# Interleaving the first two column groups of an encoder block's input projection, and moving its norm to sums per token

## The chip, the cores and the metric

The kernel runs on one core of one Trainium2 chip. The metric is the device time of one execution in microseconds (us): 1427.27 as the median of three runs (1427.24 to 1427.72).

## What is computed

One layer of an encoder block for 256 tokens of width 2048, in float32. The part that matters here is its first line, the RMSNorm and the input projection, of which the three hyena parts of 1024 columns each come first, and the small network that makes the hyena filter:

```python
h = rms_norm(x, g_mix)                        # 256 x 2048
proj = einsum('bld,de->ble', h, w_in)         # w_in: 2048 x 10240
q, k, v, hy, gates = split(proj, ...)
hy = dwconv3(hy, hy_conv_w, hy_conv_b)        # width 3 along the tokens
x0, x1, hv = split(hy, 3)                     # 1024 channels each
kern = hyena_filters(...)                     # three layers sin(freq * (h @ w + b)), then @ w4, times a decay
u = x1 * hv
y_hy = x0 * (long_conv(u, kern) + u * hy_d)
...                                           # attention, gates, merge, w_out, gated MLP, last norm
```

## The kernel before

**A stream of weights.** Nearly all of the work is one list of *chunks* (`chunks`, filled by `add_group`, line 113). A chunk is up to 1024 columns of weights on 128 partitions: for a hyena group two *K-tiles* (128 rows of x's 2048 each) of 512 columns. The loop at the end of the kernel (lines 899 to 924) does for chunk `i`: start the load of chunk `i+5` into a slab `wr` (five buffers, on SP's queue), prepare chunk `i+2`, and emit the matmuls of chunk `i`. To prepare is to split the slab into a high half `wh` (a cast on ACT, line 99) and a low half `wl` (a subtraction on DVE, line 66), three buffers each. Each engine works through its own instructions in the order in which they were emitted.

**A hyena group** is 512 output channels over all 16 K-tiles of x, channel-major: four PSUM banks (`acc{i}_0` to `_3`), each with 128 channels on the partitions. Per K-tile and bank there are two matmuls: `wh` against x's high and low half in one (512 columns), `wl` against x's high half (256 columns) into the bank's second half; `emit_mm`, line 159. When the last chunk of a group is emitted, its four *steps* go on a list (`pending`), and `flush` takes one from it per chunk: `merged_sum` (line 187) adds a bank's halves (ACT copies one as `lo`, DVE adds), the sum is multiplied by `rstd`, and `dwconv` makes the convolution (one ACT operation, two on DVE). There are six such groups: for each half of the channels the parts 1 (x1), 2 (hv) and 0 (x0). PSUM has eight banks, handed out in rotation to groups, steps and background work alike. A group has 8 chunks; the very first has 12, eight with a single K-tile and four with two.

**x and its norm.** With each chunk of the first group its K-tiles of x are loaded, scaled by the gain and split into `xg` (`split_scaled`, one operation on ACT, one on DVE at line 78). For every two K-tiles ACT squares x (`x_norm_sq`, line 228) and GpSimd adds the squares to `sqacc`. Behind the group's last chunk `x_norm_end` (line 236) sums over the partitions with a matmul by ones into `rs_ps`, and `rsqrt_chain` (line 199) makes `rstd`, the factor of each token, on all partitions. The projection itself runs on x without that factor; it is multiplied in later.

**The filter in the background.** `filter_gen` (line 284) is a generator. From chunk 16 the loop calls it 0.9 times per chunk (`pace`). Its pieces in order: loads of its tables and the split of the `dft` matrices; the split of `w4` (cast on ACT, subtraction on DVE); three layers, each a small matmul into `f_ps{l}`, an ACT operation that makes `fy`, five DVE operations, and Sin on ACT, with two empty pieces behind each; a split; then the matmuls `h_ps...` with `w4`, followed by the work for the filter's spectrum.

Of the kernel before, what the change touches and what calls it, by code (L numbers as in the profile page):

```python
# [17 lines left out]
P = 128  # L18
# [28 lines left out]
def block(ctx: ExitStack, tc: tile.TileContext, a, out):  # L47
# [14 lines left out]
    def etile(tag, name, shape=(P, T), bufs=None):  # L62
        return ev.tile(list(shape), F32, tag=tag, name=name, bufs=bufs)
# [16 lines left out]
    def ts(o, x, s1, s2, op0, op1=None):  # L80
        if op1 is None:
            nc.vector.tensor_scalar(out=o, in0=x, scalar1=s1, scalar2=None, op0=op0)
        else:
            nc.vector.tensor_scalar(out=o, in0=x, scalar1=s1, scalar2=s2, op0=op0, op1=op1)
# [99 lines left out]
                    mm(o, xl, wh[:, k, :], False, end and k == n - 1)  # L184
        return g if end else None

    def merged_sum(pt, name):
        lo = etile("lo", f"lo_{name}")
        nc.scalar.copy(out=lo, in_=pt[:, T:])  # L189
        s = etile("sum", f"s_{name}")  # L190
        add(s, pt[:, :T], lo)
        return s

    def dwconv(dst, u, c0):
        act(dst, u, AF.Identity, scale=pk[:, c0 + 1:c0 + 2], bias=pk[:, c0 + 3:c0 + 4])
        stt(dst[:, 1:], u[:, :T - 1], pk[:, c0:c0 + 1], dst[:, 1:], ALU.mult, ALU.add)
        stt(dst[:, :T - 1], u[:, 1:], pk[:, c0 + 2:c0 + 3], dst[:, :T - 1], ALU.mult, ALU.add)

    def rsqrt_chain(dst, src, n, name):

        b = etile("sq", f"rq_{name}", (P, 2, T), 2)
        ms, t = b[:, 0, :n], b[:, 1, :n]
        ts(ms, src, 1.0 / D, EPS, ALU.mult, ALU.add)
        act(t, ms, AF.Sqrt)
        nc.vector.reciprocal(out=dst, in_=t)
        mul(t, dst, dst)
        mul(t, t, ms)
        ts(t, t, -0.5, 1.5, ALU.mult, ALU.add)
        mul(dst, dst, t)


    xT = [s8(f"xT{i}", [P, 8, T]) for i in range(2)]
# [13 lines left out]
        return xT[kk // 8][:, kk % 8, :]  # L226

    def x_norm_sq(j):
        sq = etile("sq", f"sq{j}", (P, 2, T), 2)
        act(sq, xT[j // 4][:, (j % 4) * 2:(j % 4) * 2 + 2, :], AF.Square)  # L230
        if j == 0:
            nc.gpsimd.tensor_copy(out=sqacc, in_=sq)
        else:
            nc.gpsimd.tensor_tensor(out=sqacc, in0=sqacc, in1=sq, op=ALU.add)

    def x_norm_end():
        pt = bank("rs_ps")
        nc.gpsimd.tensor_tensor(out=sqacc[:, 0, :], in0=sqacc[:, 0, :], in1=sqacc[:, 1, :], op=ALU.add)
        mm(pt[:, :T], ones, sqacc[:, 0, :], True, True)
        rsqrt_chain(rstd, pt[:, :T], T, "x")  # L240
        d = etile("cv", "rtok")
        for t in range(2):
            nc.vector.tensor_tensor_reduce(out=d[:, :P], in0=rstd[:, t * P:(t + 1) * P], in1=ident, scale=1.0,
                                           scalar=0.0, op0=ALU.mult, op1=ALU.add,
                                           accum_out=rstd_tok[:, t:t + 1])

    def xop(kk):
        return xg[kk // 4][:, kk % 4, :]
# [4 lines left out]
    def hy_groups():  # L253
        def eo(x):
            return x.rearrange("p (m e) -> p e m", e=2)

        def step(part, half, c):
            def f(pts):
                ct = half * 4 + c
                if part == 1 and c == 0:  # L260
                    hy["x1"] = s8(f"hy_x1_{half}", [P, 4, T])
                    if half == 0:
                        hy["u"] = s8("hy_u", [P, 8, 2, P])
                        hy["x0"] = s8("hy_x0", [P, 8, T])
                s = merged_sum(pts[c], f"hy{part}_{ct}")
                mul(s, s, rstd)
                c0 = C_HYC + 4 * (part * 8 + ct)
                if part == 0:
                    dwconv(hy["x0"][:, ct, :], s, c0)
                elif part == 1:  # L270
                    dwconv(hy["x1"][:, c, :], s, c0)
                else:
                    v = etile("cv", f"hv{ct}")
                    dwconv(v, s, c0)
                    mul(hy["u"][:, ct, :, :], eo(hy["x1"][:, c, :]), eo(v))
            return f

        for half in range(2):
            for part in (1, 2, 0):
                first = part == 1 and half == 0  # L280
                add_group(a["w_in"][6 + part * 2 + half], KT, 512, xop, [step(part, half, c) for c in range(4)],
                          sizes=[1] * 8 + [2] * 4 if first else None)

    def filter_gen():
        raw = s8("dft_raw", [P, 8, P])
# [546 lines left out]
        while bg:  # L832
            run_bg(1)

    pair, pace = [False], [0.9, 0.0]

    def setp(pr, pc):
        pair[0], pace[0] = pr, pc
# [60 lines left out]
    for i in range(n):  # L899
        if i in events:  # L900
            flush(9)
            for fn in events[i]:
                fn()
        if i + LOAD < n:
            load(i + LOAD)
        if i + SPLIT < n:
            prep(i + SPLIT)
        if i == 6:
            nc.sync.dma_start(out=pk[:, C_HYC:], in_=a["pk"][:, C_HYC:])
        if i == 16:  # L910
            bg.append(filter_gen())
        g = emit_mm(i)
        if i == 11:
            x_norm_end()
        flush(1)
        pace[1] += pace[0]
        while pace[1] >= 1:
            pace[1] -= 1
            run_bg(1)
        if g is not None:  # L920
            pts = g.pts
            g.pts = None
            pending += [lambda f=f, pts=pts: f(pts) for f in g.steps]
            flush(1)
    while pending:
        pending.pop(0)()
    assert not bg
# [108 lines left out]
```

## Time and profile before

| | us |
|---|---|
| median of three runs | 1427.27 |
| the profiled execution, its own time | 1428.48 |
| its span, first to last instruction | 1426.2 |
| PE (TensorE's matmuls) busy | 1412.1 |
| PEld (its weight loads, beside PE) busy | 1214.2 |
| DVE (VectorE) busy | 991.6 |
| ACT (ScalarE) busy | 782.4 |
| POOL (GpSimd) busy | 19.2 |
| granted TensorE clock, mean | 0.998 |

Busy times are sums over the whole span, so they tell which engine is full and not where it stands idle; the chain of waits and the timelines tell that. SP only issues transfers. In rows of the trace `out<-in` are the names of tiles with buffer numbers left out, `128x512` is partitions x elements, and `[0.98 <-ACT wh]` at a row's end is the idle time of the engine ahead of it and what ended that. DVE and ACT records that follow each other overlap by some 0.08 us: an operation's record ends after the next one's has begun.

### The profile page before, as it was taken

What the parts mean: (1) busy time and instruction counts of PE and PEld (TensorE: products, weight loads), DVE (VectorE), ACT (ScalarE), POOL (GpSimd) and SP (SyncE); (2) the same over time, 40 slices, a digit from 0 to 9 for tenths busy, and PEclk for the clock granted to TensorE, in tenths of its full rate; (3) what the DMA queues carried; (4) which work ended last, traced back from release to release, by engine and by line L of the source; (5) the groups of instructions that cost most, each with busy time, mean ns of one, the idle gap of its engine ahead of it and who ended that gap; (6) DMA issues with size and microseconds to landing.
All of it is one profiled execution on the core that took longest, in us unless ns stands there. A gap on an engine that the chain in (4) does not pass through costs nothing.

```text
span 1426.2 us, 20169 instructions
## 1 busy us (share of the span) xinstructions
PE 1412.1 (99%) x7588; PEld 1214.2 (85%) x7588; DVE 991.6 (70%) x1532; ACT 782.4 (55%) x1171; POOL 19.2 (1%) x35
## 2 busy tenths in 40 slices
PE   8999999999999999999999999999999999999997
PEld 6888888888888888888888888888888888888897
DVE  7988877755688765755677787777777776545464
ACT  7665554443576666444566566565655654434354
POOL 3000000000000000000000000000000000000000
PEclk9999999999999999999999999999999999999999
DMA  8755555566555557565556666666666666666683
GB/s 276 240 185 156 164 175 176 165 224 195 187 163 161 165 174 239 177 189 180 184 188 191 191 191 191 188 189 190 191 190 192 190 190 221 195 193 192 192 262 123
DMA packets 77866, 271.88 MB, mean 191 GB/s; under 512 B 8960, under 2 KB 12065, under 8 KB 77257
## 3 DMA queue, kind: packets, MB, share of 16 engines
q1 hardware_dynamic: 77048, 269.54, 60.3%
q8 instruction: 59, 0.97, 0.3%
q10 hardware_dynamic: 720, 1.07, 0.2%
q14 instruction: 39, 0.31, 0.1%
HBM read 268.45 MB, written 2.11 MB: 190 GB/s over the span
## 4 chain that ended last, share of the span: by engine, by line
PE 98%; DMA 1%; DVE 1%; issue 0%; SPq 0%; ACT 0%; DVEq 0%; ACTq 0%
PE acc L90 94%; DMA wr<-in_w_in_dram 1%; PE s_ps L90 1%; PE y_ps L90 1%; PE o_ps L90 0%; DVE wl L66 0%; PE h_ps L90 0%; PE k_ps L90 0%; PE mt L475 0%; PE wt_ps L621 0%; PE xt L475 0%; PE ua_ps L90 0%; PE ub_ps L90 0%; PE ut_ps L376 0%; PE ot_ps L668 0%
## 5 line engine op out<-in xcount | busy, mean ns | idle before, releaser
L66 DVE TENSOR_TENSOR wl<-wr,wh 128x1024 fp32r<-128x1024 f32 (+1 forms) x495 | 602.4, 1218 | 378.0 <-ACT wh L99 376.1
L99 ACT CAST wh<-wr 128x1024 fp32r<-128x1024 f32 (+1 forms) x495 | 516.9, 1045 | 521.1 <-PE acc L90 474.5
L90 PE MATMUL acc<-xg,wh 128*128 128x512 f32 x2048 | 715.0, 395 | 1.5 <-ACT wh L99 1.3
L90 PE MATMUL acc<-xg,wl 128*128 128x256 f32 x2048 | 567.1, 278 | 2.7 <-DVE wl L66 2.5
L90 PEld LDWEIGHTS acc<-xg,wh 128*128 128x128 f32 x2048 | 383.6, 188 | 91.0 <-ACT wh L99 2.2
L90 PEld LDWEIGHTS acc<-xg,wl 128*128 128x128 f32 x2048 | 384.5, 188 | 6.4 <-DVE wl L66 5.0
L90 PE MATMUL acc<-wh,m 128*128 128x512 f32 (+1 forms) x832 | 218.2, 350 | 0.0
L90 PE MATMUL acc<-wh,xg 128*128 128x512 f32 x640 | 205.2, 393 | 0.0
L90 PEld LDWEIGHTS acc<-wh,m 128*128 128x128 f32 x832 | 146.9, 189 | 20.5
L90 PE MATMUL acc<-wl,m 128*128 128x512 f32 (+1 forms) x416 | 145.7, 350 | 0.0
L90 PEld LDWEIGHTS acc<-wh,xg 128*128 128x128 f32 x640 | 120.2, 188 | 24.6 <-issue 0.2
L90 PE MATMUL acc<-wl,xg 128*128 128x512 f32 x320 | 124.8, 390 | 0.0
L90 PEld LDWEIGHTS acc<-wl,m 128*128 128x128 f32 x416 | 78.7, 189 | 10.5 <-DVE wl L66 0.2
L90 PE MATMUL acc<-wh,mg 128*128 128x512 f32 x256 | 81.2, 393 | 0.0
L90 PEld LDWEIGHTS acc<-wl,xg 128*128 128x128 f32 x320 | 60.2, 188 | 11.7 <-DVE wl L66 0.2
L90 PEld LDWEIGHTS acc<-wh,mg 128*128 128x128 f32 x256 | 48.1, 188 | 9.9
L90 PE MATMUL acc<-wl,mg 128*128 128x512 f32 x128 | 49.8, 389 | 0.0
L90 PE MATMUL acc<-wh,att 128*128 128x512 f32 x128 | 41.4, 395 | 0.0
L78 DVE SCALAR_TENSOR_TENSOR sg<-s_up,pk,sg 128x255 f32<-128x255 f32 x88 | 39.5, 480 | 1.0 <-ACT sg L87 0.2
L78 DVE SCALAR_TENSOR_TENSOR vv<-s_up,pk,vv 128x255 f32<-128x255 f32 x88 | 39.3, 478 | 0.4
L90 PE MATMUL acc<-wh,yhy 128*128 128x512 f32 x128 | 39.6, 389 | 0.0
L189 ACT COPY lo_up<-acc 128x256 f32<-128x256 f32 x88 | 32.1, 365 | 10.7 <-PE acc L90 9.3
(198 smaller groups left out, 970.6 us busy)
## 6 DMA issues: line engine op xcount, KB each, us to landing
wr<-in_w_up_dram SPq DMA_DIRECT2D x176, 512.0 KB, 4.2
wr<-in_w_in_dram SPq DMA_DIRECT2D x156, 512.0 KB, 3.8
wr<-in_w_down_dram SPq DMA_DIRECT2D x66, 512.0 KB, 4.3
wr<-in_w_out_dram SPq DMA_DIRECT2D x32, 512.0 KB, 3.6
wr<-in_w_down_t_dram SPq DMA_DIRECT2D x28, 512.0 KB, 4.7
wr<-in_w_hb_dram SPq DMA_DIRECT2D x16, 512.0 KB, 4.4
wr<-in_w_ab_dram SPq DMA_DIRECT2D x16, 512.0 KB, 4.2
wr<-in_w_in_dram SPq DMA_DIRECT2D x8, 256.0 KB, 5.1
```

The source lines that it names most:

```text
L66: nc.vector.tensor_tensor(out=o, in0=x, in1=y, op=op)
L78: nc.vector.scalar_tensor_tensor(out=o, in0=x, scalar=s, in1=y, op0=op0, op1=op1)
L90: nc.tensor.matmul(o, lhsT=lhsT, rhs=rhs, start=start, stop=stop)
L99: nc.scalar.copy(out=hi, in_=x)
L189: nc.scalar.copy(out=lo, in_=pt[:, T:])
```

## The change

Part 1 and part 2 of the first half of the channels are now the first two groups, and their chunks alternate in the list: chunk 0 of the one, chunk 0 of the other, and so on, each group with four chunks of one K-tile and six of two (20 chunks in all). The eight banks of PSUM hold both groups. Since a pair of chunks shares its K-tiles, x is loaded and split with every other chunk. The remaining order is part 0, then parts 1, 2 and 0 of the second half.

The squares are added by DVE, GpSimd adds none. When the two groups end, their sums are *parked* without the norm's factor, in places of `hy_x1` and `hy_u` that are free until later (up to four steps at once while the chunk number is under 20). Then comes the norm as a step (`x_norm_chain`): two f32 matmuls of 128 columns give the sums per token on the partitions, the arithmetic is done on 128x2 values, and DVE writes two diagonal matrices into `sqacc`; two steps later `x_norm_spread` brings them to all partitions by a matmul of 256 columns and a copy on ACT. The convolutions of the parked sums follow as steps. The filter starts at chunk 23 and is called 1.15 times per chunk.

```diff
--- before.py
+++ after.py
@@ -184,10 +184,10 @@
                     mm(o, xl, wh[:, k, :], False, end and k == n - 1)
         return g if end else None
 
-    def merged_sum(pt, name):
+    def merged_sum(pt, name, s=None):
         lo = etile("lo", f"lo_{name}")
         nc.scalar.copy(out=lo, in_=pt[:, T:])
-        s = etile("sum", f"s_{name}")
+        s = etile("sum", f"s_{name}") if s is None else s
         add(s, pt[:, :T], lo)
         return s
 
@@ -195,18 +195,6 @@
         act(dst, u, AF.Identity, scale=pk[:, c0 + 1:c0 + 2], bias=pk[:, c0 + 3:c0 + 4])
         stt(dst[:, 1:], u[:, :T - 1], pk[:, c0:c0 + 1], dst[:, 1:], ALU.mult, ALU.add)
         stt(dst[:, :T - 1], u[:, 1:], pk[:, c0 + 2:c0 + 3], dst[:, :T - 1], ALU.mult, ALU.add)
-
-    def rsqrt_chain(dst, src, n, name):
-
-        b = etile("sq", f"rq_{name}", (P, 2, T), 2)
-        ms, t = b[:, 0, :n], b[:, 1, :n]
-        ts(ms, src, 1.0 / D, EPS, ALU.mult, ALU.add)
-        act(t, ms, AF.Sqrt)
-        nc.vector.reciprocal(out=dst, in_=t)
-        mul(t, dst, dst)
-        mul(t, t, ms)
-        ts(t, t, -0.5, 1.5, ALU.mult, ALU.add)
-        mul(dst, dst, t)
 
 
     xT = [s8(f"xT{i}", [P, 8, T]) for i in range(2)]
@@ -226,23 +214,33 @@
         return xT[kk // 8][:, kk % 8, :]
 
     def x_norm_sq(j):
-        sq = etile("sq", f"sq{j}", (P, 2, T), 2)
+        sq = sqacc if j == 0 else etile("sq", f"sq{j}", (P, 2, T), 2)
         act(sq, xT[j // 4][:, (j % 4) * 2:(j % 4) * 2 + 2, :], AF.Square)
-        if j == 0:
-            nc.gpsimd.tensor_copy(out=sqacc, in_=sq)
-        else:
-            nc.gpsimd.tensor_tensor(out=sqacc, in0=sqacc, in1=sq, op=ALU.add)
-
-    def x_norm_end():
+        if j:
+            add(sqacc, sqacc, sq)
+        if j == 7:
+            add(sqacc[:, 0, :], sqacc[:, 0, :], sqacc[:, 1, :])
+
+    def x_norm_chain(pts):
         pt = bank("rs_ps")
-        nc.gpsimd.tensor_tensor(out=sqacc[:, 0, :], in0=sqacc[:, 0, :], in1=sqacc[:, 1, :], op=ALU.add)
+        for t in range(2):
+            mm(pt[:, t * P:(t + 1) * P], sqacc[:, 0, t * P:(t + 1) * P], ones, True, True)
+        rq = cp.tile([P, 2, 2], F32, name="rq")
+        ms, y = rq[:, 0, :], rq[:, 1, :]
+        ts(ms, pt[:, 0:2 * P:P], 1.0 / D, EPS, ALU.mult, ALU.add)
+        act(y, ms, AF.Sqrt)
+        nc.vector.reciprocal(out=rstd_tok, in_=y)
+        mul(y, rstd_tok, rstd_tok)
+        mul(y, y, ms)
+        ts(y, y, -0.5, 1.5, ALU.mult, ALU.add)
+        mul(rstd_tok, rstd_tok, y)
+        for t in range(2):
+            ts(sqacc[:, 0, t * P:(t + 1) * P], ident, rstd_tok[:, t:t + 1], None, ALU.mult)
+
+    def x_norm_spread(pts):
+        pt = bank("rd_ps")
         mm(pt[:, :T], ones, sqacc[:, 0, :], True, True)
-        rsqrt_chain(rstd, pt[:, :T], T, "x")
-        d = etile("cv", "rtok")
-        for t in range(2):
-            nc.vector.tensor_tensor_reduce(out=d[:, :P], in0=rstd[:, t * P:(t + 1) * P], in1=ident, scale=1.0,
-                                           scalar=0.0, op0=ALU.mult, op1=ALU.add,
-                                           accum_out=rstd_tok[:, t:t + 1])
+        nc.scalar.copy(out=rstd, in_=pt[:, :T])
 
     def xop(kk):
         return xg[kk // 4][:, kk % 4, :]
@@ -254,15 +252,24 @@
         def eo(x):
             return x.rearrange("p (m e) -> p e m", e=2)
 
-        def step(part, half, c):
+        def parked(part, c):
+            return hy["x1"][:, 4 + c, :] if part == 1 else hy["u"][:, 4 + c, :, :].rearrange("p e m -> p (e m)")
+
+        def park(part, c):
+            def f(pts):
+                if part == 1 and c == 0:
+                    hy["x1"] = s8("hy_x1_0", [P, 8, T])
+                    hy["u"] = s8("hy_u", [P, 8, 2, P])
+                    hy["x0"] = s8("hy_x0", [P, 8, T])
+                merged_sum(pts[c], f"hy{part}_{c}", parked(part, c))
+            return f
+
+        def step(part, half, c, early=False):
             def f(pts):
                 ct = half * 4 + c
-                if part == 1 and c == 0:
+                if part == 1 and c == 0 and not early:
                     hy["x1"] = s8(f"hy_x1_{half}", [P, 4, T])
-                    if half == 0:
-                        hy["u"] = s8("hy_u", [P, 8, 2, P])
-                        hy["x0"] = s8("hy_x0", [P, 8, T])
-                s = merged_sum(pts[c], f"hy{part}_{ct}")
+                s = parked(part, c) if early else merged_sum(pts[c], f"hy{part}_{ct}")
                 mul(s, s, rstd)
                 c0 = C_HYC + 4 * (part * 8 + ct)
                 if part == 0:
@@ -275,11 +282,15 @@
                     mul(hy["u"][:, ct, :, :], eo(hy["x1"][:, c, :]), eo(v))
             return f
 
-        for half in range(2):
-            for part in (1, 2, 0):
-                first = part == 1 and half == 0
-                add_group(a["w_in"][6 + part * 2 + half], KT, 512, xop, [step(part, half, c) for c in range(4)],
-                          sizes=[1] * 8 + [2] * 4 if first else None)
+        sizes = [1] * 4 + [2] * 6
+        add_group(a["w_in"][8], KT, 512, xop, [park(1, c) for c in range(4)], sizes=sizes)
+        add_group(a["w_in"][10], KT, 512, xop,
+                  [park(2, c) for c in range(4)] + [x_norm_chain, lambda pts: None, x_norm_spread]
+                  + [step(part, 0, c, True) for part in (1, 2) for c in range(4)], sizes=sizes)
+        n0 = len(sizes)
+        chunks[:] = [c for pr in zip(chunks[:n0], chunks[n0:]) for c in pr]
+        for part, half in ((0, 0), (1, 1), (2, 1), (0, 1)):
+            add_group(a["w_in"][6 + part * 2 + half], KT, 512, xop, [step(part, half, c) for c in range(4)])
 
     def filter_gen():
         raw = s8("dft_raw", [P, 8, P])
@@ -832,7 +843,7 @@
         while bg:
             run_bg(1)
 
-    pair, pace = [False], [0.9, 0.0]
+    pair, pace = [False], [1.15, 0.0]
 
     def setp(pr, pc):
         pair[0], pace[0] = pr, pc
@@ -907,11 +918,9 @@
             prep(i + SPLIT)
         if i == 6:
             nc.sync.dma_start(out=pk[:, C_HYC:], in_=a["pk"][:, C_HYC:])
-        if i == 16:
+        if i == 23:
             bg.append(filter_gen())
         g = emit_mm(i)
-        if i == 11:
-            x_norm_end()
         flush(1)
         pace[1] += pace[0]
         while pace[1] >= 1:
@@ -921,7 +930,7 @@
             pts = g.pts
             g.pts = None
             pending += [lambda f=f, pts=pts: f(pts) for f in g.steps]
-            flush(1)
+            flush(4 if i < 20 else 1)
     while pending:
         pending.pop(0)()
     assert not bg
```

Three places where the order of an engine's instructions changes. The rows are the engine's instructions in its own order; a number behind a name is that of the chunk (`wl5`), K-tiles group (`xg1`) or bank, and the last number of a name only tells tiles apart.

DVE at the start, from the low half of chunk 3 on, before:

```order
L66 TENSOR_TENSOR wl3_162<-wr3_102,wh3_161 128x512
L78 SCALAR_TENSOR_TENSOR xg1_78<-xT0_75,pk_72,xg1_78 128x256
L66 TENSOR_TENSOR wl4_182<-wr4_105,wh4_181 128x512
L78 SCALAR_TENSOR_TENSOR xg1_78<-xT0_75,pk_72,xg1_78 128x256
L66 TENSOR_TENSOR wl5_199<-wr5_136,wh5_198 128x512
L78 SCALAR_TENSOR_TENSOR xg1_78<-xT0_75,pk_72,xg1_78 128x256
L66 TENSOR_TENSOR wl6_219<-wr6_157,wh6_218 128x512
```

and from chunk 4's on after the change:

```order
L66 TENSOR_TENSOR wl4_173<-wr4_103,wh4_172 128x512
L66 TENSOR_TENSOR wl5_188<-wr5_128,wh5_187 128x512
L78 SCALAR_TENSOR_TENSOR xg0_77<-xT0_75,pk_72,xg0_77 128x256
L66 TENSOR_TENSOR sqacc_81<-sqacc_81,sq1_207 128x512
L66 TENSOR_TENSOR wl6_204<-wr6_150,wh6_203 128x512
L66 TENSOR_TENSOR wl7_222<-wr7_168,wh7_221 128x512
L78 SCALAR_TENSOR_TENSOR xg1_78<-xT0_75,pk_72,xg1_78 128x256 x2
L66 TENSOR_TENSOR sqacc_81<-sqacc_81,sq2_243 128x512
L66 TENSOR_TENSOR wl8_240<-wr8_185,wh8_239 128x1024
```

Before, an operation on `xg` (a K-tile of x) stands between any two low halves. After, two low halves follow each other, and the additions into `sqacc` stand among them, where before GpSimd had them.

ACT around the filter's first layer, before (`fy0` and `fy1` are the arguments of the first and second Sin, `fsm` takes Sin's result, `hv` are convolutions):

```order
L87 ACTIVATE fy0_629<-f_ps0_627,fsm_562,pk_72 128x256
L189 COPY lo_hy2_0_659<-acc12_0_427 128x256
L189 COPY lo_hy2_1_695<-acc12_1_428 128x256
L189 COPY lo_hy2_2_727<-acc12_2_429 128x256
L189 COPY lo_hy2_3_759<-acc12_3_430 128x256
L99 CAST wh22_671<-wr22_579 128x1024
L87 ACTIVATE hv0_664<-s_hy2_0_661,pk_72 128x256
L87 ACT_TABLE_LOAD
L87 ACTIVATE fsm_562<-fy0_629 128x256
L99 CAST wh23_707<-wr23_604 128x1024
L87 ACTIVATE hv1_700<-s_hy2_1_697,pk_72 128x256
L87 ACTIVATE hv2_732<-s_hy2_2_729,pk_72 128x256
```

and after:

```order
L87 ACTIVATE fy0_790<-f_ps0_788,fsm_715,pk_72 128x256
L99 CAST wh29_826<-wr29_732 128x1024
L189 COPY lo_hy0_0_950<-acc20_0_606 128x256
L189 COPY lo_hy0_1_990<-acc20_1_607 128x256
L189 COPY lo_hy0_2_1020<-acc20_2_608 128x256
L99 CAST wh30_870<-wr30_761 128x1024
L87 ACT_TABLE_LOAD
L87 ACTIVATE fsm_715<-fy0_790 128x256
L87 ACTIVATE hv1_863<-hy_u_552,pk_72 128x256
L87 ACTIVATE hv2_895<-hy_u_552,pk_72 128x256
L87 ACTIVATE fy1_854<-f_ps1_852,fsm_715,pk_72 128x256
```

Before, between `fy0` and Sin stand four copies of bank halves, the cast of chunk 22, a convolution and the table load; behind Sin the casts go on (23, and below these rows 24 and 25) until `fy1`. After, between `fy0` and Sin stand the casts of chunks 29 and 30 with three copies and the table load, and between Sin and `fy1` two convolutions and no cast.

PE around the second layer's matmul `f_ps1`, before:

```order
L90 MATMUL acc20_3_678<-xg1_78,wl22_672 128x256
L90 MATMUL acc20_3_678<-xg1_78,wh22_671 128x512
L90 MATMUL acc20_3_678<-xg1_78,wl22_672 128x256
L90 MATMUL f_ps1_769<-fsm_562 128x256
L90 MATMUL acc20_0_675<-xg1_78,wh23_707 128x512
L90 MATMUL acc20_0_675<-xg1_78,wl23_708 128x256
L90 MATMUL acc20_0_675<-xg1_78,wh23_707 128x512
L90 MATMUL acc20_0_675<-xg1_78,wl23_708 128x256
L90 MATMUL acc20_1_676<-xg1_78,wh23_707 128x512
```

and after:

```order
L90 MATMUL acc20_3_609<-xg3_80,wh27_763 128x512
L90 MATMUL acc20_3_609<-xg3_80,wl27_764 128x256
L90 MATMUL acc20_3_609<-xg3_80,wh27_763 128x512
L90 MATMUL acc20_3_609<-xg3_80,wl27_764 128x256
L90 MATMUL f_ps1_852<-fsm_715 128x256
L90 MATMUL acc28_0_874<-xg0_77,wh28_800 128x512
L90 MATMUL acc28_0_874<-xg0_77,wl28_801 128x256
L90 MATMUL acc28_0_874<-xg0_77,wh28_800 128x512
L90 MATMUL acc28_0_874<-xg0_77,wl28_801 128x256
L90 MATMUL acc28_1_875<-xg0_77,wh28_800 128x512
```

The matmul stood behind chunk 22 and ahead of chunk 23; it now stands behind chunk 27 and ahead of chunk 28. The first layer's matmul `f_ps0` stands behind chunk 18 before and behind chunk 25 after, so that four chunks lay between the two, and two do now.

## Rows read from the trace of the kernel before

**Rows 1.** The page, section 1: busy us, share of the span, instructions, by engine.

```profile
PE 1412.1 (99%) x7588; PEld 1214.2 (85%) x7588; DVE 991.6 (70%) x1532; ACT 782.4 (55%) x1171; POOL 19.2 (1%) x35
```

**Rows 2.** Waits of PE over the span: us in total, times, longest.

```profile
PE acc L90 <- DVE wl L66: 2.5, 3, 1.4
```

**Rows 3.** The chain that ended last: start us, us, what (x of instructions).

```profile
4.03 6.35 DMA wr<-in_w_in_dram
...
11.85 5.19 DMA wr<-in_w_in_dram
...
34.21 0.43 PE rs_ps L90 x2
34.65 19.42 PE acc L90 x112
...
54.50 11.10 PE acc L90 x64
...
66.03 8.33 PE acc L90 x48
...
74.78 13.87 PE acc L90 x80
...
697.73 719.95 PE acc L90 x4072
```

**Rows 4.** Timeline of PE at the start: start us, us, engine, line, operation, [idle before].

```profile
4.97 1.29 PE L90 MATMUL acc<-xg,wh 128*128 128x512 f32 x4
...
11.15 0.98 PE L90 MATMUL acc<-xg,wh 128*128 128x512 f32 x3 [0.83 <-ACT wh L99]
```

**Rows 5.** Timelines of GpSimd (POOL) and DVE, 19 to 30 us.

```profile
19.66 1.32 POOL L234 TENSOR_TENSOR sqacc<-sqacc,sq 128x512 f32<-128x512 f32 x1 [0.50 <-ACT sq L87]
...
19.76 2.30 DVE L66 TENSOR_TENSOR wl<-wr,wh 128x1024 fp32r<-128x1024 f32 x1
...
24.96 2.38 DVE L78 SCALAR_TENSOR_TENSOR xg<-xT,pk,xg 128x256 fp32r<-128x256 f32 x2
...
28.40 0.87 DVE L78 SCALAR_TENSOR_TENSOR xg<-xT,pk,xg 128x256 fp32r<-128x256 f32 x2
29.19 1.21 DVE L66 TENSOR_TENSOR wl<-wr,wh 128x1024 fp32r<-128x1024 f32 x1
```

**Rows 6.** Timeline of ACT at the start, and one window of all engines (clock, DMA).

```profile
10.48 0.62 ACT L99 CAST wh<-wr 128x512 fp32r<-128x512 f32 x1 [0.98 <-DMA wr<-in_w_in_dram]
...
20.00:22.00 2.00, 0.75 (x4) 0.27 (x2) 2.00 (x2) 2.00 (x5) 0.98 (x1) 1.00 1.04 403
```

**Rows 7.** Groups by form, 0 to 160 us: busy us, mean ns of one, idle before.

```profile
L66 DVE TENSOR_TENSOR k<-k_ps,kt 128x512 f32<-128x512 f32 x8 | 5.5, 687 | 2.4 <-PE k_ps L90 2.4
...
L78 DVE SCALAR_TENSOR_TENSOR hy_x<-s_hy,pk,hy_x 128x255 f32<-128x255 f32 x24 | 10.7, 478 | 0.0
...
L66 DVE TENSOR_TENSOR s_hy<-s_hy,rstd 128x256 f32<-128x256 f32 x22 | 8.9, 418 | 0.1
...
L84 DVE TENSOR_SCALAR fy<-fy 128x256 f32<-128x256 f32 x6 | 1.7, 286 | 0.2 <-ACT fy L87 0.2
```

**Rows 8.** Timeline of ACT around the filter's layers.

```profile
60.81 1.28 ACT L87 ACT_TABLE_LOAD   x1
62.10 0.42 ACT L87 ACTIVATE fsm<-fy 128x256 f32<-128x256 f32 x1
...
77.48 1.05 ACT L99 CAST wh<-wr 128x1024 fp32r<-128x1024 f32 x1 [1.66 <-PE acc L90]
78.44 0.41 ACT L87 ACTIVATE fsm<-fy 128x256 f32<-128x256 f32 x1
```

**Rows 9.** Timelines of SP's queue and ACT, the filter's transfers.

```profile
43.11 0.43 SPq L286 DMA_DIRECT2D dft_raw<-in_dft_dram  x1
...
54.42 1.05 ACT L99 CAST w<-w4r 128x1024 fp32r<-128x1024 f32 x1 [1.17 <-DMA w4r<-in_hy_f_w_dram]
```

**Rows 10.** Window of all engines behind the last matmul.

```profile
1422.00:1424.00 2.00, 0.00 (x0) 0.00 (x0) 0.00 (x0) 0.00 (x0) 0.00 (x0) 0.50 1.09 351
```


## The prediction

> **What bounds the kernel now.** I read the page's engine line first: PE is busy for 1412.1 of a span of 1426.2 us [rows 1], so only time in which PE stands still, or works that it is given or spared, can move the result. The list of waits says where it stands: its largest entry is the low half of a weight slab, `wl`, made by DVE [rows 2]. The chain in order of time says when: up to 34.21 it passes through transfers, ACT and DVE, and from there on it is matmuls alone [rows 3]. So the start is the one stage with something to win. Its size: 112 matmuls (7 chunks of 16) took 19.42 us [rows 3], so a chunk of two K-tiles costs 2.775 us and a K-tile 1.387. The first group has 16 K-tiles, 22.2 us; its first matmul starts at 4.97 [rows 4] and the norm's matmul `rs_ps`, next behind its last chunk, at 34.21 [rows 3]. The start loses 34.21 - 4.97 - 22.2 = 7.05 us.
>
> Two things make that loss. Early, transfers: ACT waited 0.98 us for chunk 3's slab at 10.48 [rows 6], which had taken 6.35 us from its issue at 4.03 [rows 3]. Later, DVE: while GpSimd adds one square tile (19.66 to 20.98), a `wl` of 1024 columns takes 2.30 us instead of 1.21, and a pair of `xg` operations 2.38 instead of 0.87 [rows 5]. With GpSimd adding, a round of two K-tiles took DVE some 3 us, more than PE's 2.775.
>
> **What the change does to the start.** Two groups now share every K-tile of x, so PE has 5.55 us of work for a pair of K-tiles where it had 2.775. DVE must do for it: the `xg` pair 0.79 (0.87 less the 0.08 or so by which records in a row overlap), two `wl` at 1.14, and one addition of squares of 512 columns at 0.61 (0.687 less the overlap [rows 7]): 3.7 us of 5.55. The eight additions that move to it (some 4.6 us in all) are hidden by that slack; without it they would cost what they take. ACT needs 3.3 us of the 5.55 (two casts at 1.05, two scaled copies at 0.41, a Square of 512 columns at about the 0.62 of a cast of that size, less the overlap [rows 6, 8]). The transfers must bring 1.31 MB in 5.55 us, 236 GB/s; the queue has moved 403 GB/s in this kernel [rows 6]. So the steady part should run at PE's pace.
>
> Three chunks should still be late. Chunk 0 needs the same two transfers as before and starts at 4.97. Chunk 2's slab is the fifth transfer instead of the sixth but behind more bytes: 0.4 us. Chunk 4's slab is now the eighth; the eighth landed just before 10.48 [rows 3, 6], its cast takes 0.62, and PE wants it at about 10.9: 0.2 us. Chunk 8 is the first of 512 KB; its load waits for the buffer that `wl3` frees, at about 10, takes 5.19 to 6.35 us [rows 3], and then a cast of 1.05 and a `wl` of 1.21 (a second matmul already needs it): ready at 17.5 to 18.6, where PE is free at about 16.7 and has one matmul of 0.2 to do first. I take the later end, since 256 KB of x go ahead of it: 1.7 us. Together 2.3 us stay lost; bounds 0.7 (all of it early) and 4.7 (2.0 us for the first chunks of each group, by which chunk 3 was late before, 11.15 [rows 4] against 4.97 + 3 x 1.387, and chunk 8's at less than half its price).
>
> **What it adds on PE.** The norm's 256 columns in plain f32 cost 0.43 us [rows 3]. Now two of 128 columns (0.43 together) and one of 256 to spread the result: +0.43 us. The tiny operations on 128x2 and the two diagonals lie on DVE and ACT between the two, and two chunks (5.55 us) cover them; the removed work on 256 columns gives DVE back time that PE never waited for after 34.21 [rows 3].
>
> Parking the eight sums puts eight ACT copies and eight DVE additions behind the last two chunks. Group A's banks are wanted again at chunk 20, one chunk (2.775 us) after its last matmul; the four copies need 1.3 us (0.41 each less the overlap [rows 8]) and the additions keep pace, so I cost this at nothing. Without that cover it would be up to 1.5 us. The bank of every later group is free by its turn, as the eight are handed out in rotation.
>
> **What moves later: the filter.** filter_gen starts at chunk 23 instead of 16 and runs at 1.15 pieces per chunk. Its three sine layers are a serial loop PE, ACT, DVE, ACT, PE, and PE executes in order. Before, 64, 48 and 80 slab matmuls lay between a layer's matmul and the next consumer (11.10, 8.33 and 13.87 us) [rows 3], and that hid it: the first layer's Sin ended at 62.52 and the third's at 78.85 [rows 8], 8.0 and 4.1 us behind its matmul's end. Now the order leaves 32, 48 and 48. The first gap, 5.55 us, is shorter than the longer lag.
>
> How long PE waits at `f_ps1` I read from ACT's order: ahead of the first Sin now stand the cast of chunk 30 and a table load. That cast needs the buffer of `wh27`, and so the last `wh27` matmul, three places ahead of `f_ps1`. In the trace the same kind of cast started at 77.48, 0.07 before its chunk's end (74.78 + 2.775), and let the next operation begin at 78.44 [rows 3, 8]. So PE stands for 0.96 - 0.07 + 1.28 (load) + 0.42 (Sin) = 2.6 us. Nothing covers it: chunk 28 is queued behind `f_ps1`. Bounds: 2.0 and 4.0, since the fy chain on DVE ends only shortly before and could end later.
>
> The next wait is `h_ps000`, behind chunk 33. Count from the end of chunk 22. DVE has, from `wl25` to the end of the third layer's arithmetic, 12 operations of 1024 columns at 1.14, 17 tensor_tensor of 256 and 6 short stt at 0.335, 20 stt of 255 at 0.40 and 9 tensor_scalar at 0.205 [rows 5, 7]: 31.2 us of unbroken work, begun at about 1.0. ACT then needs 2.6 us (Sin, cast of chunk 35, two conv activations, the split): 34.8. PE arrives after 11 chunks (30.5), four f32 matmuls (1.7) and the 2.6 us: 34.8. DVE has thus become as late as PE in this stretch. For the low half of the split, 0.2 us later, and for breaks in 31 us of DVE work, I take 0.7 us; bounds 0 and 2.5, as ACT has waited 1.17 us for the filter's w4r once already [rows 9].
>
> **Sum.** 7.05 - 2.3 - 0.43 - 2.6 - 0.7 = 1.0 us gained. The profiled execution took 1428.48 us, 2.3 more than its span and 1.2 more than the median; the gain is a stretch of time alone, so I take it off the median: 1427.27 - 1.0 = 1426.3 us. Of the 4.75 us that the start gains, 3.7 are given back, 3.3 of them at the filter. One measurement of this kernel can tell about 0.2% (2.85 us) from no change, so this is "the same"; its own range, from the spread of the first and last terms, is 1424.6 to 1428.1.
>
> **Rivals.** *The gain mostly stays.* The start loses 0.7 and DVE runs without a break: 7.05 - 0.7 - 0.43 - 2.6 = 3.3 us, 1424.0. For it: DVE was slowed only while GpSimd worked [rows 5]. Against: chunk 8's 512 KB.
>
> *The start stays bound by transfers*, 4.7 us lost: 1428.7. For it: the 6.35 us [rows 3]. Against: 403 GB/s later [rows 6].
>
> *The filter's weights land late.* This ends slower. ACT casts `w4` ahead of chunk 27's slab. From the issue of `dft_raw` to that cast passed 11.3 us [rows 9]; now two slab loads, each waiting for a free buffer, stand between on SP's queue. I put the cast 7.8 us after chunk 22 at the latest and chunk 27's `wl` at 10.9, against PE's arrival at 12.0 (four chunks and two f32 matmuls at 0.43). Beyond 1.1 us more, PE waits at chunk 27 one for one: 4 us more give 1430.3. Against: ACT's wait there was 1.17 us.
>
> *The clock falls in the gap at f_ps1.* The granted clock was 1.00 over the longest wait of the start [rows 6]; at the end of the span, where the last matmul ends at 1417.68 [rows 3], it was 0.50 only from 1422 on [rows 10]. A gap of 2.6 us is shorter. If it fell to 1.2 GHz for two chunks, they would take (estimate, each twice 2.775) 5.5 us more: 1431.8. The Trainium skill, "TensorE: Matmul & The Clock Gate", section "Why this matters for your kernels", warns against idle gaps between bursts of matmuls, because the clock falls back; by this rule the interleaving's new gap is the place to look at.
>
> *The switch of tables holds ACT longer than its record*, by as much again: 1427.6. Against: Sin starts 0.01 us behind the load [rows 8]. The Trainium skill, "ScalarE: Activation LUTs", section "What ACT_TABLE_LOAD costs", adds a drain of about 1380 ns to each load's 1283 ns; the trace has the 1.28 and shows no drain behind it. By the page the sum would end at 1427.7.
>
> *The change doesn't do what it says*: the order shows the interleaving, the eight banks and no GpSimd addition, so I give this nothing.
>
> **How the numbers follow.** Forecast 1426.3: 0.62. Gain stays: 0.17. Transfers: 0.10. Late weights: 0.06. Clock: 0.03. Tables: 0.02. Faster is the second case, 0.17; slower the fourth and fifth, 0.09; the same 0.74. The range 1423.7 to 1429.5 takes in the forecast's bounds, the gain and the transfers, and leaves out late weights and clock and the ends of the others, not over 0.2.
>
> **What would show it.** In the changed profile: `rs_ps` near 54 us with no DVE record stretched over its length; PE waiting once at chunk 8; a wait of PE at `f_ps` for ACT of 2.6 us near 78 us and one at `h_ps` of under 1 us near 96; no other wait up to the first `ut_ps`. I am wrong if that `f_ps` wait isn't there (then the gain is over 3 us), if PE waits at several chunks of the start, or if the clock drops.

## The result and the profile after

The changed kernel takes 1436.11 us as the median of four runs (1434.62 to 1436.57), against 1427.26 before: a ratio of 1.0058 (95% interval 1.0045 to 1.0070). It is slower by 8.9 us, where I had forecast 1.0 us faster, and lies outside the range. The profiled execution took 1434.62 us, with a span of 1432.8.

The page's engine line after, to be held against [rows 1]: PE is busy 8.1 us longer with four matmuls more.

```profile
PE 1420.2 (99%) x7592; PEld 1220.0 (85%) x7592; DVE 989.4 (69%) x1538; ACT 781.5 (55%) x1172; POOL 6.9 (0%) x26
```

PE's waits after (engine, line, tile waited for: us in total, times, longest), against [rows 2]:

```profile
PE f_ps L90 <- ACT fsm L87: 2.7, 1, 2.7
PE warm L90 <- DVE ones L892: 1.1, 1, 1.1
PE ua_ps L90 <- DVE uq L66: 0.3, 1, 0.3
```

The waits of PE for `wl` are gone, and one new wait of 2.7 us has come, at the second filter layer. Nothing in this list is worth 8.9 us. The chain after, at the start and around the filter (start us, us, what), against the first rows of [rows 3]:

```profile
4.84 12.23 PE acc L90 x65
...
17.10 36.10 PE acc L90 x207
53.20 0.44 PE rs_ps L90 x4
53.64 5.56 PE acc L90 x32
59.20 0.43 PE rd_ps L90 x2
59.63 8.34 PE acc L90 x48
...
76.68 0.70 PE f_ps L90 x2
77.38 8.32 PE acc L90 x48
...
94.47 0.52 PE h_ps L90 x2
```

The first matmul on x, in PE's timeline (start us, us, engine, line, operation):

```profile
4.56 1.65 PE L90 MATMUL acc<-xg,wh 128*128 128x512 f32 x3
```

The size of the start's loss is near the forecast: from 4.56 on, 34 K-tiles (20 interleaved chunks and one of the next group, 34 x 1.387 = 47.2 us) lie ahead of the norm's matmul, and it begins at 53.20, so 1.5 us are lost. PE stops ahead of 76.68. And the last row of the chain, which answers to the last row of [rows 3]:

```profile
695.31 729.12 PE acc L90 x4072
```

Here the time is. When this stretch begins the changed kernel is 2.4 us ahead of the profiled execution before (695.31 against 697.73); then the same 4072 matmuls take 729.12 us instead of 719.95. PE waits for nothing in either, and the granted clock is 1.00 in both. The up groups in it, 22 groups of 64 pairs of matmuls (one of 512 columns, one of 256), run at a slower even pace; 9.17 us over 1408 pairs is 6.5 ns for each. The rest of the stretch, the down projection, is as fast as before: 227 us of it (1197 to 1424) hold 1250 matmuls, and 227 us before the change (1190 to 1417) 1249.

The edit had not touched that stretch. But it had allocated one tile more, `rq`, of 16 bytes per partition, which the allocator rounds up to 32. In the program's addresses every tile behind it, the slabs, their halves, `xg` and the rest, begins 32 bytes behind a multiple of 64, where before each began at one; two of the four `xg` tiles have also swapped places.

### The profile page after: what moved, and what is told of

Read it like the earlier page. It is cut to its first block, busy times and chain, and to the rows that moved or that the text cites. A ratio compares the mean times of both kernels' runs of the same rounds, so it can differ in the third digit from the quotient of the medians.

```text
span 1432.8 us, 20179 instructions
## 1 busy us (share of the span) xinstructions
PE 1420.2 (99%) x7592; PEld 1220.0 (85%) x7592; DVE 989.4 (69%) x1538; ACT 781.5 (55%) x1172; POOL 6.9 (0%) x26
## 4 chain that ended last, share of the span: by engine, by line
PE 99%; DVE 1%; ACT 0%; issue 0%; DVEq 0%
PE acc L90 94%; PE s_ps L90 1%; PE y_ps L90 1%; PE o_ps L90 0%; PE h_ps L90 0%; PE k_ps L90 0%; DVE wl L66 0%; PE warm L90 0%; PE mt L486 0%; PE xt L486 0%; PE wt_ps L632 0%; PE ua_ps L90 0%; PE ub_ps L90 0%; PE ut_ps L387 0%; PE ot_ps L679 0%; DVE hy_x L78 0%
## 5 line engine op out<-in xcount | busy, mean ns | idle before, releaser
L90 PE MATMUL acc<-xg,wh 128*128 128x512 f32 x2048 | 725.4, 399 | 0.0
L90 PE MATMUL acc<-xg,wl 128*128 128x256 f32 x2048 | 574.3, 281 | 0.0
```

Source lines behind the costliest of these rows:

```text
L90: nc.tensor.matmul(o, lhsT=lhsT, rhs=rhs, start=start, stop=stop)
```

## The experiments

### Alignment or places

Three kernels. `a_align` is the changed kernel with a longer `rq`:

```diff
-        rq = cp.tile([P, 2, 2], F32, name="rq")
-        ms, y = rq[:, 0, :], rq[:, 1, :]
+        rq = cp.tile([P, 2, 8], F32, name="rq")
+        ms, y = rq[:, 0, :2], rq[:, 1, :2]
```

> The changed kernel; only rq, the new 16-byte tile of the norm, is made 64 bytes long (32 unused), so that every tile allocated behind it begins at a multiple of 64 bytes in its partition again, as before the change, instead of 32 behind one. Theory 1, the new tile's size: a pair of matmuls of the up groups (768 columns) goes back from 0.352 to 0.346 us, and the time from 1436.1 to 1425.5 to 1427. Theory 2, the places that the tiles changed among each other (two xg tiles have swapped, the squares' and sums' buffers too), or another cause: 0.352 us and 1436 stay.

`b_shift32` and `b_shift64` are the kernel before with a longer `rstd_tok`:

```diff
-    rstd_tok = cp.tile([P, 2], F32, name="rstd_tok")
+    rstd_tok = cp.tile([P, 10], F32, name="rstd_tok")
```

(18 instead of 10 for `b_shift64`.)

> The kernel before, with rstd_tok made 40 bytes long instead of 8 (the rest unused): all tiles behind it move by 32 bytes, nothing else changes. Theory 1 (alignment): a pair of matmuls in the up groups takes 0.352 us instead of 0.346 and the time rises by some 9 us, to 1436. Theory 2 (places among each other): 1427.3.

> The kernel before, with rstd_tok 72 bytes long: all tiles behind it move by 64 bytes. Theory 1 (alignment to 64 bytes): no change, 1427.3. If it were the absolute place of the tiles rather than the alignment, it would move too, by up to the 9 us.

Measured: `a_align` 1427.76 us (ratio to before 1.0001, interval 0.9992 to 1.0010), `b_shift32` 1436.68 (1.0065, 1.0050 to 1.0080), `b_shift64` 1427.38 (1.0001, 0.9992 to 1.0010). The last rows of the chains, first `b_shift32`:

```profile
696.83 729.12 PE acc L90 x4072
```

then `b_shift64`, with the norm's matmul at its start:

```profile
33.09 0.43 PE rs_ps L90 x2
...
696.40 719.96 PE acc L90 x4072
```

and `a_align`, with the norm's and the second filter layer's:

```profile
53.53 0.44 PE rs_ps L90 x4
...
77.11 1.22 PE f_ps L90 x2
78.33 9.32 PE acc L90 x48
...
697.17 719.99 PE acc L90 x4072
```

The stretch of 4072 matmuls takes 729.12 us in both kernels whose tiles are 32 bytes off and 719.96 to 719.99 where they are not. 32 unused bytes in the old kernel cost it 9.2 us; 48 more in the new one give 8.4 back. The swapped `xg` tiles play no part, nor does the absolute place: `a_align` keeps the swap, and `b_shift64` moves every tile. Nor do the banks: `b_shift32` has the order of instructions and the PSUM banks of the kernel before. Theory 1 stands; that `a_align` lies 0.8 us above its expected range has probably another cause, which comes with the filter below.

### Which operand, and how

I then moved only one pool. `b_xg32` has 32 bytes ahead of the pool of 8 KB buffers (x, `xg`, the up groups' results) and 32 ahead of the small tiles behind it, so that only the big ones are off:

```diff
+    epad = big.tile([P, 8], F32, tag="pad", name="epad", bufs=1)
+    nc.gpsimd.memset(epad, 0.0)
+    vpad = ev.tile([P, 8], F32, tag="pad", name="vpad", bufs=1)
+    nc.gpsimd.memset(vpad, 0.0)
```

> The kernel before, with two unused tiles of 32 bytes (written once by GpSimd at the start): only the tiles of the pool of 8 KB buffers (x, xg, the up groups' results) begin 32 bytes behind a multiple of 64; slabs, halves and small tiles stay at multiples. Theory 1a, the moving operand xg is what must be aligned: 0.353 us for a pair of matmuls in the up groups, some 1436 us. Theory 1b, the stationary operand (slab halves): 0.3467 us and 1427.

`b_slab32` has `rstd_tok` as in `b_shift32` and `epad` alone, so that only the slabs and their halves are off.

> The kernel before, with only the slabs wr and their halves wh and wl 32 bytes behind a multiple of 64, all else at multiples. Theory 1a (xg): 0.3467 us for a pair of matmuls in the up groups, 1427 us. Theory 1b (slab halves): 0.353 us and 1436.

Both theories missed: 1439.21 and 1438.73 us, single runs, beside 1427.73 for the kernel before. Each is slower than with everything off, and elsewhere. Rows of `b_xg32`'s chain (72 matmuls of a token-major group, in which x is the stationary operand and the weights move, 64 of channel-major groups in the attention's stage, and the last stretch):

```profile
167.65 16.80 PE acc L90 x72
...
393.42 11.11 PE acc L90 x64
...
704.09 724.38 PE acc L90 x4072
```

In the kernel before, the same 72 and 64 matmuls took

```profile
168.61 16.35 PE acc L90 x72
...
390.99 11.31 PE acc L90 x64
```

and the last stretch 719.95. `b_slab32` has 16.80, 11.11 and 724.39. So where moving and stationary operand lie differently to the 64-byte grid, the token-major matmuls (512 columns) take 0.233 instead of 0.227 us each, and the channel-major pairs run at the faster pace in these rows and in the up groups, 11.11 / 32 = 0.347 us. With both off, as in the changed kernel, the token-major matmuls lose nothing:

```profile
166.30 16.35 PE acc L90 x72
```

There is no one operand that "must be aligned": for the token-major matmuls it counts how the two lie to each other, and for the channel-major pairs the case with both off is a third one.

In that third case the pace of the channel-major pairs is not a price per matmul, either. Around the filter the changed kernel, all off, runs at the fast pace (8.32 / 24 = 0.347 at 77.38), and the kernel before, all aligned, runs at 0.353 us in the attention's stage (11.31 / 32). My guess was that a pace once taken stays for hundreds of matmuls and changes at a break or at an f32 matmul. To test that, `a_kick` and `b_kick` put three f32 matmuls into the up groups, of the changed kernel and of the one before:

```diff
+        def kick(pts):
+            pt = bank("kick")
+            mm(pt[:, :T], ones, sqacc[:, 0, :], True, True)
+
         for g in range(11):
-            add_group(a["w_up"][g], KT, 512, xop, [step(g, False, c) for c in range(4)])
+            add_group(a["w_up"][g], KT, 512, xop, [step(g, False, c) for c in range(4)] + ([kick] if g in (2, 5, 8) else []))
```

> The changed kernel (tiles 32 bytes behind) with three more f32 matmuls of 256 columns in the up groups (behind the first halves of groups 2, 5 and 8), whose result nobody reads: 1.3 us of work. In the traces so far the pace of a pair, 0.3467 or 0.353 us, changes only behind such a matmul or a break in the stream. Theory A, each matmul pays for its misaligned operand: 0.353 us on both sides of each added matmul, 1437 us. Theory B, PE falls into one of two rhythms at a break and keeps it, and alignment only decides which: the pace may change at an added matmul, and the time then lies between 1428 and 1435.

> The kernel before (tiles aligned) with the same three f32 matmuls in the up groups. Theory A: 0.3467 us on both sides of each, 1428.6 us. Theory B: the pace may fall to 0.353 us behind one of them, and the time lies between 1429 and 1436.

Measured, in single runs: 1433.51 and 1428.91 us. The chain of `a_kick`:

```profile
697.34 113.07 PE acc L90 x640
810.40 0.43 PE kick L90 x2
810.84 135.68 PE acc L90 x768
946.52 0.43 PE kick L90 x2
946.95 133.13 PE acc L90 x768
```

Up to the first kick a pair takes 113.07 / 320 = 0.353 us, behind it 135.68 / 384 = 0.353, and behind the second 133.13 / 384 = 0.347, to the end of the up groups, with every tile still 32 bytes off. In `b_kick` the pace is 0.347 throughout, as theory A has it, and theory B allows that too. `a_kick` decides between them, since a price per misaligned matmul could not change at 946.52. An added matmul also takes a PSUM bank and so shifts the banks of later groups, but every second group keeps its four banks, and those too go from 0.353 to 0.347 there. So it is theory B, on one change in one execution: PE has two rhythms on this pattern, the layout decides which one it reaches at the norm's matmul ahead of the up groups, and another break may change it. All profiles and runs with everything off came out slow there, all with everything aligned fast. Why there are two rhythms, and what in the layout picks one, the profile does not show; that stays open.

### The later filter

`a_align_early` is the aligned kernel with the filter begun earlier:

```diff
-    pair, pace = [False], [1.15, 0.0]
+    pair, pace = [False], [0.9, 0.0]
...
-        if i == 23:
+        if i == 18:
             bg.append(filter_gen())
...
+        pace[0] = 1.15
         sr = s8("f_split", [P, 2, 2, T], F32R)
```

> The aligned changed kernel, with filter_gen begun at chunk 18 at 0.9 pieces per chunk (1.15 from the split behind the third layer on), so that three chunks and more lie between its layers on PE, as before the change. If the wait at the second layer's matmul (2.7 us in the changed kernel) is the whole price of the later filter, it goes, and the time is 2.4 to 2.9 us below the aligned kernel: about 1423. If the earlier start makes the filter's weights late instead, a wait of 1 to 4 us appears at a slab's cast or low half around chunks 20 to 24, and the time is that of the aligned kernel or above.

Measured: 1423.07 us, ratio 0.9968 (0.9957 to 0.9980). Its chain:

```profile
54.69 0.44 PE rs_ps L90 x4
...
57.34 0.43 PE f_ps L90 x2
...
66.64 0.43 PE f_ps L90 x2
67.07 8.33 PE acc L90 x48
...
692.90 719.94 PE acc L90 x4072
```

No wait at a filter layer is left, and no late weights have come. It is 4.7 us faster than `a_align`, though, not 2.4 to 2.9. Most of the rest was in `a_align`'s rows above: behind the gap, the second layer's matmul took 1.22 us and the next 48 matmuls 9.32, against 0.70 and 8.32 in the changed kernel's own profile, 1.5 us in all. The windows of `a_align` there (us: PE, weight loads, DVE, ACT, GpSimd busy, then the granted clock, DMA share, GB/s):

```profile
70.00:74.00 4.00, 4.00 (x25) 3.52 (x24) 4.00 (x9) 2.02 (x5) 0.00 (x0) 1.00 0.76 228
74.00:76.80 2.80, 0.36 (x3) 0.04 (x1) 2.80 (x8) 2.57 (x4) 0.00 (x0) 0.97 0.58 174
76.80:80.00 3.20, 2.89 (x8) 2.42 (x9) 3.20 (x10) 2.39 (x5) 0.00 (x0) 0.50 0.56 195
80.00:84.00 4.00, 4.00 (x25) 3.48 (x24) 2.99 (x8) 1.37 (x2) 0.00 (x0) 0.99 0.05 18
```

PE had been busy, then stood for 2.7 us, and the granted clock was 0.50, the lower of its two levels (1.2 of 2.4 GHz), from 76.8 to 80. In the changed kernel's profile the same gap left it at 1.00:

```profile
74.00:77.00 3.00, 0.32 (x1) 0.30 (x2) 3.00 (x8) 2.97 (x4) 0.00 (x0) 1.00 0.61 197
77.00:80.00 3.00, 3.00 (x19) 2.64 (x18) 3.00 (x10) 1.67 (x4) 0.00 (x0) 1.00 0.58 194
```

So the clock fell behind this gap in one profile and not in another; `a_kick`'s, with a gap of 2.7 us as well, is a second one at 1.00. In how many of `a_align`'s ten runs it fell, their mean clocks (0.997 to 0.999) don't tell: each profile also ends at a clock of 0.50, as [rows 10] show, for 5 to 8 us, and that moves the mean by as much. `a_align_fill` kept PE at work in the gap:

```diff
+            if l == 1:
+                fill = bank("fill")
+                for _ in range(6):
+                    mm(fill[:, :T], ones, sqacc[:, 0, :], True, True)
             mm(pt[:, :T], sm[:, l * P:(l + 1) * P], cur, True, True)
```

> The aligned changed kernel with six f32 matmuls of 256 columns (0.43 us each, 2.6 together; nobody reads their result) just ahead of the second filter layer's matmul, where PE stood for 2.7 us. In the profile of the aligned kernel the granted clock was 0.50 from about 76.8 to 80 us, behind that gap, and 49 matmuls there took some 1.8 us longer. If the gap brought the clock down: the clock stays at 1.00, the 1.8 us go, and the median comes to 1425.5 to 1426.5 (from 1427.8), with less spread between the runs. If the clock fell for another reason, or in that one execution alone: 1427 to 1428, as without the filling.

Measured: 1426.30 us (ratio 0.9993, 0.9984 to 1.0001), 1.5 below `a_align`. Its windows:

```profile
74.00:77.00 3.00, 2.99 (x15) 2.29 (x13) 3.00 (x8) 2.77 (x5) 0.00 (x0) 1.00 0.65 243
77.00:80.00 3.00, 2.85 (x15) 2.51 (x16) 3.00 (x10) 2.13 (x5) 0.00 (x0) 1.00 0.57 188
```

The clock stays at 1.00 in this profile, which alone would not prove much, since it did so without the filling too. The medians differ by the 1.5 us that the fall cost in `a_align`'s profile, but their intervals touch. That the gap brings the clock down is thus likely, and not shown beyond doubt. The Trainium skill, "TensorE: Matmul & The Clock Gate", section "Why this matters for your kernels", warns of idle gaps between bursts of matmuls for this reason; `a_align` agrees with it (0.50 behind 2.7 us), the profiles of the changed kernel and of `a_kick` show that it need not come.

`a_early_only` has the same earlier start without the alignment.

> The changed kernel with the earlier filter, its tiles left 32 bytes behind (rq of 16 bytes). If alignment and the filter's start are independent, it is 4.2 to 5 us faster than the changed kernel, 1431 to 1432, with 0.353 us for a pair of matmuls in the up groups. If the rhythm of PE in the up groups hangs on when the stages before it end, and not on alignment alone, the pace may come out at 0.3467 and the time at 1423.

Measured: 1432.37 us (1.0032, 1.0020 to 1.0044), 3.7 below the changed kernel, and 729.11 us for the last stretch. The filter's start leaves the pace of the up groups alone; the gain is somewhat under the 4.2 to 5 that I expected, and 2.7 of it is the wait.

### What the squares are worth

`a_early_gp` is `a_align_early` with GpSimd adding the squares again:

```diff
-            add(sqacc, sqacc, sq)
+            nc.gpsimd.tensor_tensor(out=sqacc, in0=sqacc, in1=sq, op=ALU.add)
...
-            add(sqacc[:, 0, :], sqacc[:, 0, :], sqacc[:, 1, :])
+            nc.gpsimd.tensor_tensor(out=sqacc[:, 0, :], in0=sqacc[:, 0, :], in1=sqacc[:, 1, :], op=ALU.add)
```

> The aligned kernel with the earlier filter, but with GpSimd adding the squares, as before the change. If the slack of the interleaved start (DVE has 3.7 us of work in 5.55) covers the DVE operations that GpSimd's additions stretch, then 1422.5 to 1423.5 as with DVE adding, and it is the interleaving alone that wins the start. If the stretched operations (a low half of 2.3 us instead of 1.2) still make PE wait: waits for wl in the first 50 us and 1424 to 1426.

Measured: 1423.93 us (0.9972, 0.9962 to 0.9983), 0.9 above `a_align_early`, which these intervals do not tell apart. PE waits for `wl` again, 0.2 us at the start's second chunk and 0.8 at chunk 8, so the truth lies between the two expectations:

```profile
PE acc L90 <- DVE wl L66: 1.0, 2, 0.8
```

`b_dve_sq` is the kernel before with only this:

```diff
-            nc.gpsimd.tensor_copy(out=sqacc, in_=sq)
+            pass
         else:
-            nc.gpsimd.tensor_tensor(out=sqacc, in0=sqacc, in1=sq, op=ALU.add)
+            add(sqacc, sqacc, sq)
```

(the first square goes straight into `sqacc`, and the last addition is DVE's too).

> The kernel before with DVE adding the squares and no other change (no interleaving, no new tile). If GpSimd's additions are most of what the start loses, the stretched DVE operations go, PE's waits for wl shrink from 2.5 us to under 1, and the time is 1424.5 to 1426.5. If the additions (about 0.6 us for every two K-tiles) cost DVE as much as the stretching did, because its round then takes some 2.6 of PE's 2.775 us: 1427 to 1428.5.

Measured: 1422.90 us (0.9967, 0.9955 to 0.9980). That is more than I expected and as good as the whole changed kernel with both of its faults mended. Rows of its chain:

```profile
29.46 0.43 PE rs_ps L90 x2
29.89 19.42 PE acc L90 x112
...
692.92 720.00 PE acc L90 x4072
```

and of DVE's timeline at the start:

```profile
21.26 0.87 DVE L78 SCALAR_TENSOR_TENSOR xg<-xT,pk,xg 128x256 fp32r<-128x256 f32 x2
22.06 0.68 DVE L66 TENSOR_TENSOR sqacc<-sqacc,sq 128x512 f32<-128x512 f32 x1
22.66 1.21 DVE L66 TENSOR_TENSOR wl<-wr,wh 128x1024 fp32r<-128x1024 f32 x1
23.80 0.87 DVE L78 SCALAR_TENSOR_TENSOR xg<-xT,pk,xg 128x256 fp32r<-128x256 f32 x2
```

The norm's matmul begins at 29.46, where `b_shift64`, the same start with GpSimd adding, has 33.09. A `wl` takes 1.21 us and an `xg` pair 0.87 all the time, where [rows 5] had 2.30 and 2.38 while GpSimd added; with the addition of 0.68 the round of two K-tiles takes DVE 2.54 us (21.26 to 23.80, the next pair's start), under PE's 2.775. PE waits for `wl` no more.

## Why the prediction was wrong

- **The sum.** The step that failed is the first of the prediction, "so only time in which PE stands still, or works that it is given or spared, can move the result", and with it "the gain is a stretch of time alone, so I take it off the median". Both took for granted that the matmuls which the edit doesn't touch keep their pace, a term that I put at nothing without a reason. They did not: 729.12 instead of 719.95 us, 9.2 us from a 16-byte tile, in matmuls that wait for nothing. I had compared the order of instructions and not the addresses; no rival covered it.
- **The start after the change**: 2.3 us lost, forecast; 1.5 measured (also in `a_align`: 53.53 - 4.85 - 47.2), inside the bounds. The size is near by luck: chunks 2 and 4 were not late in the changed kernel's profile, and chunk 8's `wl` by 0.2 us (17.10 instead of 16.9) where I had 1.7. Of the 1.5 us, 1.0 lies in the first eight matmuls, 4.56 to 6.96 where the pace is 1.387: those of 512 columns follow each other at 0.47 us, not at 0.23. No wait is recorded there. Matmuls behind `a_align`'s gap, at a clock of 0.50, are as slow (0.42), but no row shows the clock low at the start.
- **The start before**: the 7.05 us were read from an execution that was 1.2 us above the median, and the surplus lay in the very stage that I costed. `b_shift64`, whose time is that of the kernel before, loses 33.09 - 4.78 - 22.2 = 6.1 us there. The prize was one microsecond smaller than I took it for.
- **The wait at `f_ps1`**: 2.6 forecast, 2.7 measured, at 76.68 instead of "near 78". Right. That PE would go on at full speed behind it was not certain: the clock's fall, which I had as a rival at 0.03, came in the aligned kernel's profile, at 1.5 us rather than the 5.5 that I had priced; how often it comes stays open. Of the drain that the Trainium skill adds to a load ("ScalarE: Activation LUTs", "What ACT_TABLE_LOAD costs") nothing shows: the wait is as long as the records of the load and of Sin make it.
- **The wait at `h_ps000`**: 0.7 forecast, none measured; the lower bound.
- **The norm**: +0.43 us, as forecast: `rs_ps` 0.44 and `rd_ps` 0.43 against [rows 3]'s 0.43.
- **Late weights, transfers, table switch**: none showed. PE has no wait for a slab in the list after.

Without the misalignment the forecast's balance holds: `a_align` reaches the last stretch at 697.17, `b_shift64` at 696.40, 0.8 later; 1.5 of that is the clock, so without its fall it would have been 0.7 ahead. The start's gain and the filter's loss do cancel nearly, and the median of `a_align_fill`, 1426.30, is the number forecast. That it is met so closely is luck: the start before was 0.9 us too large in my sum, the loss of the start after 0.8 and of `h_ps000` 0.7, and these errors work against each other. With the measured terms the sum is 6.1 - 1.5 - 0.4 - 2.7 = 1.5 us gained, and where the profiles lose 0.8 of that I have not traced. I also credited the interleaving with a gain that the squares alone bring: `b_dve_sq`, without interleaving, is 4.6 us faster than the kernel before, `a_early_gp`, with interleaving and GpSimd adding, 3.6, and `a_align_early`, with both, 4.4 (the last two with aligned tiles and the earlier filter). Each part brings most of the gain by itself, and the two don't add up. I had written that DVE's round was over PE's "with GpSimd adding", and never asked what the round would be with DVE adding and nothing else: 1.14 + 0.79 + 0.61 = 2.54, from rows that I had.

## What to carry to other kernels

Compare the addresses of the tiles as well as the order of the instructions: a new tile of a few bytes can move every tile behind it, and a stage that the edit never names may change pace by 2%. Of a change with several parts, price each part alone first; here one part alone, which needed no interleaving, brought as much as all of them. And where one stage is costed from one profiled execution, see first how far that execution lies from the median, since the surplus may lie in that stage.

## What the runs showed of the hardware

- An offset of 32 bytes from a multiple of 64 in the matmuls' operands changes their pace: with all operands off, the 1408 pairs of the up groups took 9.2 us more; with only the moving or only the stationary one off, 72 token-major matmuls took 16.80 instead of 16.35 us, and with both off 16.35. The Trainium skill, "SBUF — State Buffer", section "Operand start alignment", asks for a start at a multiple of the element size and says that this is about legality and that it timed nothing; these runs put a time beside it.
- The channel-major pair has two even rhythms, 0.347 and 0.353 us, each held for hundreds of matmuls without a wait; in one run it changed at an f32 matmul between them (946.52 in `a_kick`).
- A gap of 2.7 us in PE's work was followed by a granted clock of 0.50 for 3.2 us in one profile and by 1.00 in two others of nearly the same program.
